# A kernel that plans its own order: from one planned order to twelve, each with banks and slots given by the one before

## The chip, the cores and the metric

The kernel runs on one core of one Trainium2 chip. A core has a matrix engine (TensorE, PE in the profile, with its weight loads listed apart as PEld), a vector engine (VectorE, DVE), a scalar engine (ScalarE, ACT), a general engine (GpSimd, POOL) and a synchronising engine (SP), which here issues the transfers between the main memory and the core's own memory. Each engine works through its own list of instructions in order and waits on semaphores for the others. Matrix products land in a small accumulator memory, PSUM, which has eight banks; everything else lies in SBUF.

The metric is the time of one execution on the device, in microseconds (us). The kernel before took 1474.14 us in the median of three runs (1473.09 to 1474.48).

## What is computed

A trunk of four residual layers over a sequence of 256 positions with 1024 channels. Each layer is a token mixer followed by a gated feed-forward layer (SwiGLU). The mixers are, in order, RWKV-7 time mixing, stick-breaking attention, sparse attention over selected keys (DSA), and RWKV-7 once more.

```python
for i in range(DEPTH):                     # DEPTH = 4
    kind, j = i % N_MIXERS, i // N_MIXERS  # N_MIXERS = 3
    h = rms_norm(x, norm_mix[i])
    if kind == 0:
        y, v_layer = rwkv7_time_mix(h, v_first, ...)
    elif kind == 1:
        y = stick_breaking_attention(h, sb_w_qkv[j], sb_w_out[j])
    else:
        y = dsa_attention(h, ds_w_in[j], ds_q_norm[j], ds_k_norm[j], ds_w_out[j])
    x = x + y
    x = x + swiglu(rms_norm(x, norm_ffn[i]), ffn_w_gu[i], ffn_w_down[i])
```

In the sparse attention a small indexer scores the keys for each query, the 64 best visible ones are kept, and an ordinary softmax attention with 16 heads runs over these alone. In RWKV-7 each head carries a 64 by 64 state through time:

```python
sa = einsum('bhvk,bhk->bhv', state, kk_t)
state = state * w_t - sa[..., None] * (kk_t * a_t) + v_t[..., None] * k_t
y_t = einsum('bhvk,bhk->bhv', state, r_t)
```

## The kernel before

The activations stay on the core, channels on the 128 partitions and the 256 positions along the free dimension. All weights come in 397 pieces of 128 by 1024 numbers (512 KB each), loaded into four rotating slots (`raw`). In most layers a piece is split on arrival into a rounded high part (`wh`, a cast on ScalarE or VectorE) and the rest (`wl`, a subtraction on VectorE). The products then run on the rounded halves: a pass with `wh` over the high and the low half of the activations, and one with `wl` over the high half. RWKV's r, k and v products use the unsplit piece.

The feed-forward layer makes 22 gate and 22 up products (`gate`, `up`), then eight products back to 1024 channels (`dn`). The RWKV layer makes its r, k and v products (`rp`, `kp`, `vp`), small products for its gates (`lora_in`, `lw`, `la`, `g1a`, `g1b`, `pg`), scores within chunks of 64 positions (`sc`), the inverse of a triangular matrix per head and chunk, finished by many 32 by 32 products (`cmb`), and then the recurrence over four chunks (`xu`, `qu`, `pS`, `Y`, with the state in `Sn`); the output product is `po`. The sparse attention makes the index products (`qi`, `kiwi`), keys of the index (`ki`), scores (`idx`), picks the best 64 on VectorE by eight rounds of "take the eight greatest, strike them out", and then treats eight pairs of heads: projection (`qk`), norm (`qss`), rotation (`qrot`), masked scores (`z`), softmax, transposition (`pT`), the weighted sum (`attn_o`). Value products (`vps`) and output products (`po`) are spread among them.

Nothing of this is issued directly. The layers are written as calls on a recording object, `Plan`: `record` (line 318) makes an operation (`Op`, line 179) with an estimated cost per engine, and finds from the overlap of regions in each buffer which earlier operations it needs. Some operations may go to either of two engines (`any`: a copy to ScalarE or VectorE, a product of two SBUF tiles to VectorE or GpSimd). Several matmuls may form one unit. At the end `emit` (line 650) calls `schedule` (line 630) and issues the instructions in the planned order. All instructions issued through it carry line 661, so the profile's groups are told apart by the names of their tiles.

`_prepare` (line 377) gives buffers of a group with a fixed number of slots (`ps`, five PSUM banks; `g`, two; `t`, twelve small tiles; `wh` and `wl`, three each; and single places such as `SB` or `s6`) their slot. It walks the buffers in the order in which the program recorded them, and gives each the slot whose last user stands earliest in that recorded order. The first operations on the new buffer then depend on all last reads and writes of the old one. The groups `raw` and `xm` (`FREE`, line 221) are left to the scheduling itself. Then it adds loads of ScalarE's function tables, and gives each operation a rank: its cost and the longest chain of costs and latencies behind it.

`_schedule` (line 420) is a list scheduler. It keeps a time per engine, takes the engine that can start first, and of its ready operations the one of highest rank, with some exceptions (`choose`, line 508): an engine waits for a more urgent operation that is about to be ready, goes elsewhere with an operation that another engine would finish sooner, and keeps TensorE for a while on products of one shape class, the full array or parts of it (operations whose `parts` flag is set have 64 rows or columns or fewer; a change costs `SWITCH`). Where the plan has TensorE waiting, it puts in filler (`keep_warm`, line 480): pairs of small bf16 products `warm_o` from a constant tile (`WARMERS = 2`, line 215). They compute nothing that is used; they hold the matrix engine's clock up. How many are put in follows from a count of the array's recent columns (`filled`).

In the kernel before one order is made. The `reserve` values are tried in turn until one gives a complete order.

Of the kernel before, what the change touches and what calls it, by code (L numbers as in the profile page):

```python
# [61 lines left out]
class Region:  # L62


    def __init__(self, p0, p1, cols, width):
        self.p0, self.p1 = p0, p1
        cols = np.asarray(cols).ravel()
        self.lo, self.hi = int(cols.min()), int(cols.max()) + 1
        self.mask = None
        if len(cols) < self.hi - self.lo or len(np.unique(cols)) < self.hi - self.lo:  # L70
            self.mask = np.zeros(width, bool)
            self.mask[cols] = True
# [106 lines left out]
class Op:  # L179


    def __init__(self, eng):
        self.eng, self.instrs, self.cost, self.table, self.cols = eng, [], 0.0, None, 0.0
        self.preds, self.succs, self.alts, self.warmer, self.parts = set(), [], {}, False, False
        self.bufs, self.ns = [], 0.0


class Queue:
# [27 lines left out]
ROW = 3  # L216
GAP = 1100.0
RESERVES = (1, 2, 3, 4, 5, 6)

WAIT = {"tensor": 85.0, "vector": 55.0, "scalar": 40.0, "gpsimd": 40.0, "sync": 0.0}  # L220
FREE = ("raw", "xm")
# [58 lines left out]
class Plan:  # L280
# [95 lines left out]

    def _prepare(self, counts):

        for b in self.bufs:
            if b.ops:  # L380
                b.ops = list(dict.fromkeys(b.ops))
                b.first, b.last = min(o.idx for o in b.ops), max(o.idx for o in b.ops)
        self.grouped, held = {}, {}
        for b in sorted((b for b in self.bufs if b.ops and b.group is not None), key=lambda b: b.first):
            if b.group in FREE:
                self.grouped.setdefault(b.group, []).append(b)
                for o in b.ops:
                    o.bufs.append(b)
                continue
            slots = held.setdefault(b.group, [None] * counts.get(b.group, 1))  # L390
            k = min(range(len(slots)), key=lambda i: -1 if slots[i] is None else slots[i].last)
            old = slots[k]
            if old is not None:
                assert old.last < b.first, (b.name, old.name, b.group)
                for o in b.roots:
                    o.preds |= {q for q, _ in old.writes + old.reads if q is not o}
            slots[k], b.slot = b, f"{b.group}_{k}"
        load, table, now, before = None, None, [], []
        for o in list(self.ops):
            if o.table is None:  # L400
                continue
            if o.table != table:
                table, before, now = o.table, now, []
                load = Op("scalar")
                load.cost, load.table, load.idx = 1290.0, table, o.idx - 0.5
                load.preds |= set(before)
                self.ops.append(load)
            o.preds.add(load)
            now.append(o)
        self.ops.sort(key=lambda o: o.idx)  # L410
        for o in self.ops:
            o.preds.discard(o)
            for q in o.preds:
                assert q.idx < o.idx
                q.succs.append(o)
        for o in reversed(self.ops):
            o.base = o.eng, o.cost
            o.rank = o.cost + max((s.rank + self._lat(o, s) for s in o.succs), default=0.0)

    def _schedule(self, counts, reserve):  # L420
        engines = ("tensor", "vector", "scalar", "gpsimd", "sync")
# [206 lines left out]
        return max(free.values()), sorted(out, key=lambda o: o.start)  # L628

    def schedule(self, counts):  # L630
        self._prepare(counts)
        best = None
        for reserve in RESERVES:
            r = self._schedule(counts, reserve)
            if r is not None:
                best = r
                break
        self.time, self.out = best
        Plan.last = self
        return self.out  # L640

# [1087 lines left out]
```

## Time and profile before

| | before |
|---|---|
| median of three runs | 1474.14 us |
| the profiled execution | 1473.95 us |
| its span, from the first to the last instruction | 1472.2 us |
| mean granted TensorE clock | 0.999 |
| TensorE busy | 1447.0 us |
| filler products `warm_o` | 294 |
| read from main memory | 219.70 MB |

The profile is a page on one execution, together with views that answer narrower questions: groups of instructions with their busy time and mean duration, waits by releaser, the chain that ended last, a timeline, and busy times within chosen stretches. Two points help in reading them. Matmuls are pipelined, so the duration of one is longer than the time that it takes from its successor: a feed-forward product of 512 columns is listed with 398 ns, though the next starts earlier. The time of a sequence is therefore read from start to start. And a product on full-precision (f32) numbers appears as two records, so the profile counts 10434 matmuls where the program has 8498.

### The profile page before, as it was taken

How to read it: one execution, taken by the hardware profiler on the slowest of the kernel's cores; microseconds unless marked ns; L12 is line 12 of the kernel's file. 1: busy time of each engine (PE TensorE's matmuls, PEld its weight loads, DVE VectorE, ACT ScalarE, POOL GpSimd, SP SyncE). 2: the span in 40 equal slices, each digit the busy share in tenths (PEclk: the TensorE clock that was granted, in tenths of full speed). 3: DMA queues.
4: the chain of work that ended last, by engine and by line, in shares of the span. 5: the costliest groups of instructions: out<-in, count | busy, mean ns of one | idle time of the engine just before them, and what ended most of it. 6: DMA issues, size and time to landing. Idle time of an engine off the chain costs nothing.

```text
span 1472.2 us, 26233 instructions
## 1 busy us (share of the span) xinstructions
PE 1447.0 (98%) x10434; PEld 1228.1 (83%) x10434; DVE 1107.1 (75%) x2026; ACT 718.3 (49%) x1348; POOL 61.3 (4%) x57
## 2 busy tenths in 40 slices
PE   9999999999999999999999989999999999999998
PEld 6788788888888888888977868888877877888887
DVE  7297478998566779986789978986474884789864
ACT  2344665444447655444546755444325256654442
POOL 0000010000000010000100010000100001200000
PEclk9999999999999999999999999999999999999999
DMA  7234135655554445555634445555523430455653
GB/s 254 91 107 144 36 101 172 194 183 194 175 183 136 130 158 186 198 187 181 192 113 130 129 144 172 186 193 183 197 93 108 129 101 18 130 175 182 196 188 132
DMA packets 77803, 224.55 MB, mean 153 GB/s; under 512 B 23536, under 2 KB 23792, under 8 KB 77424
## 3 DMA queue, kind: packets, MB, share of 16 engines
q1 hardware_dynamic: 77680, 222.87, 46.4%
q8 instruction: 82, 1.34, 0.4%
q14 instruction: 41, 0.34, 0.1%
HBM read 219.70 MB, written 3.15 MB: 151 GB/s over the span
## 4 chain that ended last, share of the span: by engine, by line
PE 86%; DVE 9%; ACT 2%; DMA 2%; issue 1%; SPq 0%; POOL 0%; DVEq 0%
PE up L661 17%; PE dn L661 16%; PE gate L661 16%; PE qk L661 5%; PE po L661 4%; PE kp L661 4%; PE rp L661 4%; PE vps L661 3%; PE z L661 2%; DVE wl L661 2%; PE vp L661 2%; PE warm_o L1564 1%; PE Y L661 1%; PE sc L661 1%; DVE xg L661 1%
## 5 line engine op out<-in xcount | busy, mean ns | idle before, releaser
L661 ACT CAST wh<-raw 128x1024 fp32r<-128x1024 f32 x317 | 329.7, 1050 | 401.8 <-PE dn L661 130.2
L661 DVE TENSOR_TENSOR wl<-raw,wh 128x1024 fp32r<-128x1024 f32 x349 | 420.3, 1222 | 70.0 <-ACT wh L661 58.5
L661 PE MATMUL gate<-xg,wh 128*128 128x512 f32 x704 | 259.9, 398 | 3.9 <-DVE xg L661 2.1
L661 PE MATMUL up<-xg,wh 128*128 128x512 f32 x704 | 259.9, 397 | 0.0
L661 PE MATMUL dn<-h,wh 128*128 128x512 f32 x704 | 247.6, 394 | 0.0
L661 PE MATMUL dn<-h,wl 128*128 128x256 f32 x704 | 197.5, 280 | 0.0
L661 PE MATMUL gate<-xg,wl 128*128 128x256 f32 x704 | 197.2, 280 | 0.0
L661 PE MATMUL up<-xg,wl 128*128 128x256 f32 x704 | 197.2, 280 | 0.0
L661 PEld LDWEIGHTS gate<-xg,wh 128*128 128x128 f32 x704 | 132.2, 188 | 38.1 <-DVE xg L661 3.4
L661 PEld LDWEIGHTS up<-xg,wh 128*128 128x128 f32 x704 | 132.2, 188 | 31.1
L661 PEld LDWEIGHTS dn<-h,wh 128*128 128x128 f32 x704 | 132.4, 188 | 30.8
L661 PEld LDWEIGHTS up<-xg,wl 128*128 128x128 f32 x704 | 132.8, 189 | 0.2
L661 PEld LDWEIGHTS gate<-xg,wl 128*128 128x128 f32 x704 | 132.8, 189 | 0.1
L661 PEld LDWEIGHTS dn<-h,wl 128*128 128x128 f32 x704 | 132.4, 188 | 0.0
L661 PE MATMUL qk<-xg,wh 128*128 128x256 f32 (+1 forms) x384 | 95.0, 326 | 0.1
L661 PE MATMUL qk<-xg,wl 128*128 128x256 f32 x256 | 72.0, 281 | 0.4 <-DVE wl L661 0.4
L661 PEld LDWEIGHTS qk<-xg,wh 128*128 128x128 f32 x384 | 64.2, 189 | 7.8 <-issue 1.4
L661 PE MATMUL kp<-pre,raw 128*128 128x256 f32 x256 | 59.9, 386 | 1.7 <-DVE pre L661 1.7
L661 DVE TENSOR_TENSOR gus<-gus,rstd 128x512 f32<-128x512 f32 x88 | 59.8, 687 | 1.2
L661 PE MATMUL vp<-xv,raw 128*128 128x256 f32 x256 | 59.0, 385 | 0.9 <-DVE vf L661 0.9
L661 PE MATMUL rp<-xr,raw 128*128 128x256 f32 x256 | 58.7, 382 | 0.0
L661 PEld LDWEIGHTS kp<-pre,raw 128*128 128x128 f32 x256 | 47.3, 190 | 13.3 <-issue 4.0
(292 smaller groups left out, 2355.5 us busy)
## 6 DMA issues: line engine op xcount, KB each, us to landing
raw<-in_wts_dram SPq DMA_DIRECT2D x397, 512.0 KB, 3.6
lora<-in_lora_dram SPq DMA_DIRECT2D x2, 1536.0 KB, 9.2
lg<-in_lora_dram SPq DMA_DIRECT2D x4, 512.0 KB, 5.4
xt<-in_xT_dram SPq DMA_DIRECT2D x4, 256.0 KB, 4.0
lora<-in_lora_dram SPq DMA_DIRECT2D x2, 512.0 KB, 5.6
xi<-in_id_dram SPq DMA_DIRECT2D x2, 512.0 KB, 8.0
scr<-SB SPq DMA_DIRECT2D x8, 128.0 KB, 3.4
xa<-scr SPq DMA_DIRECT2D x2, 512.0 KB, 3.3
```

Source lines behind the costliest of these rows:

```text
L661: getattr(getattr(nc, o.eng), method)(*map(real, args), **{k: real(a) for k, a in kw.items()})
L1564: lambda: [nc.tensor.matmul(wo[:, :S], wx[:, :P], wx, start=True, stop=True) for _ in range(WARMERS)])
```

## The change

`_prepare` no longer gives slots. It only collects the buffers that share a group, and keeps for each operation the needs that come from the data (`needs`) and its first engine and cost (`base`). A new function, `_place`, takes an order, sorts the buffers of each group by their first use in that order, and gives each the slot whose old buffer is finished earliest by the planned end times (`end`) of that order. It then makes the dependencies and ranks anew. `schedule` starts from the recorded order with made-up times, so that its first round gives slots as before. It repeats placing and scheduling `ROUNDS = 12` times, each round starting from the order of the round ahead of it without its fillers. By the planner's own estimate of the total time it keeps the shortest of the twelve, and restores engines, costs, instructions, times and slots of that one.

```diff
+ROUNDS = 12
...
+    def _place(self, counts, order):
+
+        at = {o: i for i, o in enumerate(order)}
+        for o in self.ops:
+            o.preds, o.succs = set(o.needs), []
+        for g, bufs in self.grouped.items():
+            bufs.sort(key=lambda b: min(at[o] for o in b.ops))
+        for g, bufs in self.placed.items():
+            slots = [None] * counts.get(g, 1)
+            for b in sorted(bufs, key=lambda b: min(at[o] for o in b.ops)):
+                k = min(range(len(slots)), key=lambda i: -1.0 if slots[i] is None else max(o.end for o in slots[i].ops))
+                old = slots[k]
+                if old is not None:
+                    for o in b.roots:
+                        o.preds |= {q for q, _ in old.writes + old.reads if q is not o}
+                slots[k], b.slot = b, f"{g}_{k}"
+        for o in self.ops:
+            o.preds.discard(o)
             for q in o.preds:
-                assert q.idx < o.idx
+                assert at[q] < at[o]
                 q.succs.append(o)
-        for o in reversed(self.ops):
-            o.base = o.eng, o.cost
-            o.rank = o.cost + max((s.rank + self._lat(o, s) for s in o.succs), default=0.0)
+        for o in reversed(order):
+            o.rank = o.base[1] + max((s.rank + self._lat(o, s) for s in o.succs), default=0.0)
...
     def schedule(self, counts):
         self._prepare(counts)
-        best = None
-        for reserve in RESERVES:
-            r = self._schedule(counts, reserve)
-            if r is not None:
-                best = r
-                break
-        self.time, self.out = best
+        order, best = self.ops, None
+        for o in order:
+            o.start, o.end = o.idx, o.idx + 0.5
+        for _ in range(ROUNDS):
+            self._place(counts, order)
+            for reserve in RESERVES:
+                r = self._schedule(counts, reserve)
+                if r is not None:
+                    break
+            if best is None or r[0] < best[0]:
+                best = r + ([(o.eng, o.cost, o.instrs, o.start, o.end) for o in r[1]], [b.slot for b in self.bufs])
+            order = [o for o in r[1] if not o.warmer]
+        self.time, self.out = best[:2]
+        for o, state in zip(best[1], best[2]):
+            o.eng, o.cost, o.instrs, o.start, o.end = state
+        for b, slot in zip(self.bufs, best[3]):
+            b.slot = slot
```

The arithmetic, the numbers of slots and banks, the cost estimates and the transfers stay as they are.

More of the change, by code (lines that the diff above doesn't have):

```diff
@@ L184, in __init__ @@
         self.preds, self.succs, self.alts, self.warmer, self.parts = set(), [], {}, False, False
-        self.bufs, self.ns = [], 0.0
+        self.bufs, self.ns, self.end = [], 0.0, 0.0
 class Queue:
@@ L377, in _prepare @@
     def _prepare(self, counts):
+        self.grouped, self.placed = {}, {}
         for b in self.bufs:
@@ L382, in _prepare @@
                 b.first, b.last = min(o.idx for o in b.ops), max(o.idx for o in b.ops)
[L383 to L397, printed above, removed]
+                if b.group in FREE:
+                    self.grouped.setdefault(b.group, []).append(b)
+                    for o in b.ops:
+                        o.bufs.append(b)
+                elif b.group is not None:
+                    self.placed.setdefault(b.group, []).append(b)
         load, table, now, before = None, None, [], []
@@ L412, in _prepare @@
             o.preds.discard(o)
+            o.needs, o.base = frozenset(o.preds), (o.eng, o.cost)
+    def _place(self, counts, order):
[15 more added lines that the diff above has]
+            o.preds.discard(o)
             for q in o.preds:
-                assert q.idx < o.idx
+                assert at[q] < at[o]
                 q.succs.append(o)
-        for o in reversed(self.ops):
-            o.base = o.eng, o.cost
-            o.rank = o.cost + max((s.rank + self._lat(o, s) for s in o.succs), default=0.0)
+        for o in reversed(order):
+            o.rank = o.base[1] + max((s.rank + self._lat(o, s) for s in o.succs), default=0.0)
     def _schedule(self, counts, reserve):
```

## The prediction

> **What bounds the kernel now.** I read the page first, then busy time by stage, then the filler passes by stage, then TensorE's waits and its timeline. The page says whose time it is.
>
> ```profile
> span 1472.2 us, 26233 instructions
> PE 1447.0 (98%) x10434; PEld 1228.1 (83%) x10434; DVE 1107.1 (75%) x2026; ACT 718.3 (49%) x1348; POOL 61.3 (4%) x57
> PE 86%; DVE 9%; ACT 2%; DMA 2%; issue 1%; SPq 0%; POOL 0%; DVEq 0%
> ```
>
> TensorE (PE) is busy nearly always and holds 86% of the chain that ended last. But part of that busy time computes nothing: the passes named warm_o, which the planner puts where its own plan has TensorE waiting. Cut at the first gate product and the last dn product of each feed-forward layer, the span has eight stages; five are shown (RWKV, a feed-forward layer, stick-breaking, sparse attention, RWKV):
>
> ```profile
> core 0: us, PE busy (x) PEld busy (x) DVE busy (x) ACT busy (x) POOL busy (x), PEclk, DMA share, GB/s
> 1.20:219.40 218.20, 214.28 (x2134) 172.03 (x2135) 142.57 (x358) 103.17 (x277) 12.09 (x13) 1.00 0.38 123
> 219.40:407.20 187.80, 187.19 (x1062) 162.69 (x1063) 152.05 (x223) 88.66 (x114) 6.18 (x4) 1.00 0.56 184
> 407.20:525.70 118.50, 117.76 (x786) 101.98 (x783) 82.61 (x136) 75.13 (x148) 3.45 (x3) 1.00 0.46 147
> ...
> 712.50:876.20 163.70, 155.80 (x1139) 133.74 (x1137) 138.62 (x282) 97.57 (x218) 9.68 (x8) 1.00 0.43 138
> ...
> 1070.90:1280.80 209.90, 206.88 (x2097) 165.94 (x2097) 144.02 (x370) 99.43 (x269) 9.95 (x10) 1.00 0.31 94
> ```
>
> The same stretches for warm_o alone:
>
> ```profile
> 1.20:219.40 218.20, 20.02 (x126) 1.00 0.38 123
> ...
> 712.50:876.20 163.70, 8.17 (x64) 1.00 0.43 138
> 876.20:1070.90 194.70, 4.26 (x36) 1.00 0.55 184
> 1070.90:1280.80 209.90, 10.81 (x64) 1.00 0.31 94
> ```
>
> The reader is to see two kinds of stage. A feed-forward layer has TensorE full (187.19 of 187.80 us) without filler: no order can shorten it. The sparse attention loses most: 8.17 us of filler and 163.70 - 155.80 = 7.9 us idle. The two RWKV stages hold 126 and 64 filler passes; the first 64 of the 126 stand ahead of the first product, while inputs load.
>
> **The change part by part.** It adds and removes no arithmetic; it changes the order, the banks and slots, and the engine of some copies. With one order instead of twelve the new planner gives exactly the old program, so all that follows comes from the later orders. In the changed kernel's instruction order (the fifth of the twelve; counts below are from it) the matmuls are the same but for warm_o, 236 instead of 294. Per stage: first RWKV 126 to 120, sparse attention 64 to 26, last RWKV 64 to 50, all others equal. The four feed-forward stages have the same sequence of products as before.
>
> *Filler.* Per pass, from the rows above: 8.17/64 = 0.128 us in the sparse attention, 10.81/64 = 0.169 in the last RWKV, 20.02/126 = 0.159 in the first. So 38 x 0.128 + 14 x 0.169 + 6 x 0.159 = 4.9 + 2.4 + 1.0 = 8.2 us. Back to back a pass takes less, about 3.88/34 = 0.114 us:
>
> ```profile
> 1.19 5.73 PE L1564 MATMUL warm_o<-warm_x 128*128 128x256 bf16 x30 [1.19 <-DVE eps_rms L661]
> 9.21 3.88 PE L1564 MATMUL warm_o<-warm_x 128*128 128x256 bf16 x34
> 20.36 3.72 PE L661 MATMUL kp<-pre,raw 128*128 128x256 f32 x16
> 24.01 1.08 PE L661 MATMUL lora_in<-xm,lora 128*64 128x256 f32 x8
> 25.02 1.99 PE L661 MATMUL kp<-pre,raw 128*128 128x256 f32 x8
> 26.95 1.08 PE L661 MATMUL lora_in<-xm,lora 128*64 128x256 f32 x8
> ```
>
> That makes the lower end 58 x 0.114 = 6.6 us. I take 8.2, because the removed passes mostly stood in pairs between dependent products, not in long runs.
>
> *Switches between the full array and parts of it.* 16 kp passes hold TensorE from 20.36 to 24.01 (3.65 us), 8 from 25.02 to 26.95 (1.93): 1.72 for eight more, 0.215 each, so each visit carries 1.93 - 8 x 0.215 = 0.21 us beside its passes, 0.10 for each of its two switches. The order before has 280 switches, the new one 246: first RWKV 108 to 102, sparse attention 38 to 34, last RWKV 110 to 86. 34 x 0.10 = 3.4 us. The lower end is nothing (a switch made while waiting is free). I take 3.4: in RWKV most switches stand amid a busy TensorE.
>
> *Waits in the sparse attention.* What TensorE waited for there, longest four:
>
> ```profile
> PE qrot L661 <- DVE rhl L661: 2.7, 4, 1.7
> PE vps L661 <- DVE wl L661: 1.5, 1, 1.5
> PE pT L661 <- DVE prs L661: 1.0, 1, 1.0
> PE qss L661 <- ACT prs L661: 0.9, 1, 0.9
> ```
>
> They stand beside the filler at two places: from the index keys (ki) to the first masked score product (z), and around the last two head pairs.
>
> ```profile
> 745.37:775.38 30.01, 26.37 (x188) 21.87 (x188) 28.82 (x84) 13.44 (x22) 1.59 (x3) 1.00 0.26 89
> 851.44:868.24 16.80, 13.84 (x96) 9.39 (x95) 8.52 (x25) 9.49 (x32) 0.00 (x0) 1.00 0.43 158
> 851.44:868.24 16.80, 5.03 (x40) 1.00 0.43 158
> 729.58 0.72 PE qk L661 x6
> 781.59 1.38 PE vps L661 x6
> ```
>
> In the first stretch VectorE (DVE) is busy 28.82 of 30.01 us with the top-k; TensorE has only 96 qk and 24 vps passes to put beside it (96 x 0.12 + 24 x 0.23 = 17.0 us). The new order has 240 qk and 48 vps passes there (39.8 us): later head pairs are projected early, so the pairs overlap afterwards. At the end, where 40 of the 64 filler passes stood, the new order has 4: output products (po) stand between the last pairs. The four rows make 6.1 us of waits, and I count them down as the filler falls, by 38/64: 3.6 us. Bounds: 0 (the same waits elsewhere) and all 6.1.
>
> *New waits.* No row shows the new order's own. The nearest is what the old planner left unfilled: 3.9 us idle in the first RWKV (218.20 - 214.28) up to 7.9 in the sparse attention. A new order may leave less as well as more; after the term above I bound it by -3.9 and +7.9 and take +3, since the new order packs the chains closer and a late link then stalls sooner.
>
> *Engine choices.* VectorE loses 7 weight casts to ScalarE and 5 rotary products to GpSimd:
>
> ```profile
> L661 DVE CAST wh<-raw 128x1024 fp32r<-128x1024 f32 x32 | 23.0, 719 | 10.4 <-PE vps L661 5.4 <-PE qk L661 2.6 <-PE xu L661 1.7
> L661 ACT CAST wh<-raw 128x1024 fp32r<-128x1024 f32 x317 | 329.7, 1050 | 401.8 <-PE dn L661 130.2
> L661 DVE TENSOR_TENSOR qk<-qa,sbt 128x512 f32<-128x512 f32 x5 | 3.5, 692 | 0.2
> L661 POOL TENSOR_TENSOR qk<-qa,sbt 128x512 f32<-128x512 f32 x3 | 4.3, 1428 | 49.2 <-DVE qa L661 42.5 <-PE qk L661 6.7
> L661 DVE TENSOR_TENSOR wl<-raw,wh 128x1024 fp32r<-128x1024 f32 x38 | 46.9, 1238 | 4.4 <-ACT wh L661 4.2
> L661 DVE TENSOR_TENSOR qa<-qk,rstd 128x512 f32<-128x512 f32 x8 | 5.4, 681 | 0.3 <-PE qk L661 0.2
> ...
> 762.54 1.30 POOL L661 TENSOR_TENSOR qk<-qa,sbt 128x512 f32<-128x512 f32 x1 [6.70 <-PE qk L661]
> 762.71 1.68 DVE L661 CAST wh<-raw 128x1024 fp32r<-128x1024 f32 x1
> ```
>
> Each cast is 0.33 us slower, each product 0.74 us. I cost them at nothing: ScalarE is busy 97.57 of 163.70 us in that stage, and the product runs beside the split, rotation and sine product of the same pair. Uncovered they cost 7 x 0.33 + 5 x 0.74 = 6.0 us. There is a second price: the cast that began 0.17 us after a GpSimd product took 1.68 us, not 0.72, about 1.0 us late. Five more such products hold VectorE up by at most 5.0 us and spare it 5 x 0.692 = 3.5: 1.5 more VectorE time, which I leave to the rival below.
>
> "SBUF — State Buffer" of the Trainium skill, under "SBUF: two separate sides", has the reason: VectorE in a two-port mode or with two SBUF inputs and GpSimd hold that pair exclusively for a whole instruction, and the other blocks. By that rule each product may cost VectorE its full 1.43 us, 3.7 us net for five; the pair of rows agrees in kind.
>
> DMA issues are the same in number; where one moves, the DMA share (0.31 to 0.56) leaves room.
>
> *The sum.* 1472.2 - 8.2 - 3.4 - 3.6 + 3.0 = 1460.0 us of span. The profiled run took 1473.95, 1.75 outside the span; the median of the runs shown is 1474.14, 0.2 above it. Forecast 1462.0 us. Its own range: all 6.1 us of waits gone and no new ones gives 1456; filler at 6.6, no gain from switches or waits, and the 3 us lost gives 1470.5.
>
> **The rivals.**
>
> *VectorE takes over in the sparse attention (slower).* The first stretch gets 144 more qk passes (six weight pieces) and 24 more vps passes (two pieces): eight splits of 1.238 us and three evictions of 0.681 on VectorE, 28.8 + 11.9 = 40.7 us, against TensorE's 39.8. For it: VectorE is already full there, the mask stands behind all of that on its queue, and GpSimd's five products delay it by 1.5 us more. Against it: the work is only moved ahead, and the stage's total on VectorE (138.62 of 163.70) falls. It decides once the mask is later than the prefilled products; then pairs run on their own chain as the last two did, 16.80 us with 13.84 - 5.03 = 8.8 of work, 8.0 us lost per two pairs. Twice that on top of the forecast is 1478.
>
> *Waits stay, filler goes.* The removed passes leave idle time of the same length: only part of the switches remains, 1472. For it: filler alone never sets a time. Against it: the work between dependent products visibly changes.
>
> *The recurrences gain too.* The new order starts the state recurrence (xu, qu, pS, Y) amid the inverse's products (cmb) instead of behind most of them. In this stretch of the first RWKV:
>
> ```profile
> 150.00:172.00 22.00, 22.00 (x509) 16.12 (x511) 6.94 (x21) 13.71 (x52) 0.00 (x0) 1.00 0.11 39
> 150.00:172.00 22.00, 9.02 (x54) 1.00 0.11 39
> ```
>
> 9.02 of 22 us is filler, hiding latency. Half of it saved in both layers is 9 us more: 1453. Against it: the new order still holds 50 fillers in the last RWKV.
>
> *The clock falls.* Fewer fillers could cost clock. The first 30 passes took 5.73 us, 0.19 each, against 0.114 later: a cold stretch of that length costs 5.73 - 30 x 0.114 = 2.3 us, and six of them eat the gain, 1475. Against it: every stage shows 1.00, across waits of up to 1.7 us. "TensorE: Matmul & The Clock Gate" of the Trainium skill, under "What's actually happening", has the clock halved after an idle window of about 3.4 us; no wait here is as long.
>
> That the change does nothing is out: the sequences differ.
>
> **How the numbers follow.** Forecast 0.64, VectorE 0.11, waits stay 0.11, recurrences 0.12, clock 0.02. The range reaches below to just under the recurrences' 1453 and above past "waits stay" to the clock's 1475: 1452 to 1475, leaving out most of VectorE and the tails. A difference of 0.2% (2.9 us) is what a measurement of this kernel tells from none. Faster: forecast 0.63, recurrences 0.12, a third of "waits stay" 0.04: 0.79. Same: the rest of "waits stay" and a piece of VectorE and of the forecast: 0.11. Slower: 0.10.
>
> **What would show it.** Right: feed-forward stages at 187 us again, the sparse attention near 153, the last RWKV some 5 us shorter, clock 1.00 throughout. Wrong: the sparse attention's TensorE idle above 8 us with VectorE near 95% of it; an RWKV stage longer than before; or the filler gone with idle time grown by as much.

## The result, and the profile after

The changed kernel takes 1464.55 us in the median of six runs (1462.82 to 1465.98), against 1474.31 for the kernel before on the same chip (1473.09 to 1475.66): a ratio of 0.9932, 95% interval 0.9919 to 0.9945. The forecast was 1462.0 in a range of 1452 to 1475. The page of the changed kernel begins like this:

```profile
span 1462.9 us, 26102 instructions
PE 1440.6 (98%) x10376; PEld 1222.8 (84%) x10376; DVE 1104.9 (76%) x2034; ACT 720.2 (49%) x1334; POOL 70.6 (5%) x63
PE 88%; DVE 8%; ACT 2%; issue 1%; DMA 1%; SPq 0%; POOL 0%; DVEq 0%; ACTq 0%
```

The span is 9.3 us shorter, and TensorE bounds it as before. Busy times cut at the same events (columns: length, then busy time and count of PE, PEld, DVE, ACT and POOL, granted clock, DMA share, GB/s) show where:

```profile
1.20:217.30 216.10, 213.74 (x2128) 170.69 (x2129) 144.05 (x362) 102.16 (x273) 12.84 (x13) 1.00 0.38 125
...
405.10:523.70 118.60, 117.91 (x785) 102.03 (x783) 84.27 (x139) 75.30 (x145) 3.44 (x3) 1.00 0.46 147
...
710.50:866.90 156.40, 150.54 (x1101) 130.26 (x1099) 130.39 (x270) 102.24 (x225) 18.39 (x13) 1.00 0.44 145
...
1062.10:1271.60 209.50, 205.81 (x2082) 165.14 (x2083) 146.29 (x380) 96.94 (x258) 9.82 (x11) 0.99 0.31 94
```

The sparse attention fell from 163.7 to 156.4 us and gives four fifths of the gain. The first RWKV fell by 2.1, the last by only 0.4; stick-breaking and the feed-forward layers stayed within 0.5. The filler products alone, in the stages where they changed:

```profile
1.20:217.30 216.10, 19.95 (x120) 1.00 0.38 125
...
710.50:866.90 156.40, 3.36 (x26) 1.00 0.44 145
...
1062.10:1271.60 209.50, 7.87 (x50) 0.99 0.31 94
```

Over the whole span filler went from 44.0 to 36.2 us. TensorE's idle time went from 25.2 (1472.2 - 1447.0) to 22.3 (1462.9 - 1440.6). What is left, TensorE busy with real products, rose from 1403.0 to 1404.4. So -7.8 - 2.9 + 1.4 = -9.3. The rise stands in the last RWKV, shown here in three parts, before and after: from its first product to the first score product (`sc`), on to the first product of the inverse (`cmb`), and on to its end. First the kernel before:

```profile
1070.90:1143.60 72.70, 72.68 (x360) 55.28 (x360) 44.25 (x112) 28.16 (x72) 0.90 (x1) 1.00 0.30 95
1143.60:1211.90 68.30, 67.25 (x671) 54.75 (x670) 57.91 (x164) 26.37 (x69) 0.00 (x0) 1.00 0.39 115
1211.90:1280.80 68.90, 66.95 (x1071) 55.92 (x1069) 41.87 (x96) 44.90 (x128) 9.04 (x9) 1.00 0.23 71
```

Then the changed kernel:

```profile
1062.10:1136.70 74.60, 74.43 (x364) 54.88 (x364) 46.69 (x118) 28.67 (x72) 1.12 (x1) 1.00 0.30 92
1136.70:1205.90 69.20, 67.53 (x665) 55.38 (x664) 55.75 (x156) 27.69 (x72) 0.00 (x0) 0.98 0.38 114
1205.90:1271.60 65.70, 63.85 (x1054) 54.87 (x1055) 43.84 (x108) 40.58 (x115) 8.69 (x10) 1.00 0.24 74
```

The beginning of the first part on the changed kernel's TensorE timeline (start, duration):

```profile
1063.92 0.38 PE L1589 MATMUL warm_o<-warm_x 128*128 128x256 bf16 x2
1064.13 2.13 PE L686 MATMUL kp<-pre,raw 128*128 128x256 f32 x8
1066.10 0.38 PE L1589 MATMUL warm_o<-warm_x 128*128 128x256 bf16 x2
1066.41 0.65 PE L686 MATMUL lora_in<-xm,lora 128*64 128x256 f32 x4
1067.05 1.13 PE L686 MATMUL kp<-pre,raw 128*128 128x256 f32 x4
1068.11 0.65 PE L686 MATMUL lora_in<-xm,lora 128*64 128x256 f32 x4
1068.69 1.13 PE L686 MATMUL kp<-pre,raw 128*128 128x256 f32 x4
```

The recurrence at the end gained 3.2 us. The first part, where TensorE hardly waits, lost 1.9: four fillers that were not there before, and `lora_in` products mostly in groups of four passes where the old order had groups of eight, each group paying two changes of array mode. The middle lost 0.9 us, and its clock column reads 0.98. Two stretches of it, of 3.4 us each:

```profile
1167.69:1171.11 3.42, 3.42 (x8) 2.76 (x9) 3.35 (x12) 3.40 (x10) 0.00 (x0) 0.50 0.05 19
1171.11:1174.52 3.41, 3.41 (x17) 3.00 (x17) 3.13 (x9) 0.73 (x1) 0.00 (x0) 1.00 0.00 0
```

In the first the granted clock is half, and 8 products stand in it instead of 17: the profiled execution lost some 1.7 us there (3.42 x 0.5, an estimate). With these set aside real products fell by about 0.3 us instead of rising by 1.4, and the middle lost nothing through its order. At its end stands TensorE's longest wait of the stage, on VectorE (us, times, longest):

```profile
PE cmb L686 <- DVE xd L686: 1.2, 1, 1.2
```

### The profile page after: what moved, and what is told of

The parts are those of the page before. It is cut to its first block, busy times and chain, and to the rows that moved or that the text cites. A ratio compares the mean times of both kernels' runs of the same rounds, so it can differ in the third digit from the quotient of the medians.

```text
span 1462.9 us, 26102 instructions
## 1 busy us (share of the span) xinstructions
PE 1440.6 (98%) x10376; PEld 1222.8 (84%) x10376; DVE 1104.9 (76%) x2034; ACT 720.2 (49%) x1334; POOL 70.6 (5%) x63
## 4 chain that ended last, share of the span: by engine, by line
PE 88%; DVE 8%; ACT 2%; issue 1%; DMA 1%; SPq 0%; POOL 0%; DVEq 0%; ACTq 0%
PE up L686 17%; PE dn L686 17%; PE gate L686 16%; PE qk L686 5%; PE vp L686 4%; PE rp L686 4%; PE kp L686 4%; PE vps L686 3%; PE po L686 3%; PE z L686 2%; DVE wl L686 2%; PE sc L686 1%; DVE xg L686 1%; PE Y L686 1%; PE warm_o L1589 1%
## 5 line engine op out<-in xcount | busy, mean ns | idle before, releaser
L686 ACT CAST wh<-raw 128x1024 fp32r<-128x1024 f32 x324 | 338.1, 1050 | 415.3 <-PE dn L686 130.3
L686 PE MATMUL kp<-pre,raw 128*128 128x256 f32 x256 | 63.4, 389 | 2.0 <-DVE pre L686 1.7
```

The costliest lines, as they stand in the source:

```text
L686: getattr(getattr(nc, o.eng), method)(*map(real, args), **{k: real(a) for k, a in kw.items()})
```

## The experiments

My theory going in: the planner now needs less waiting, above all in the sparse attention, and the fillers mark how much. Its rival: the filler products themselves cost the time, so that any kernel with fewer of them is faster. The kernel before ran beside each of the following on the same chip; the ratios and intervals are to those runs.

### Is filler idle time, or does it delay?

Edits, in the changed kernel (`half_after`, `none_after`) and in the kernel before (`half_before`, `none_before`):

```diff
-              lambda: [... for _ in range(WARMERS)])
+              lambda: [... for _ in range(WARMERS // 2)])                        # half
+              lambda: [... for _ in range(WARMERS if next(calls) < 32 else 0)])  # none after the start
```

> The order before, with one filler product where the plan has two (147 instead of 294; 63 of the 147 removed stand ahead of the first weight product). Theory 1, filler only stands where TensorE would wait anyway: within 2 us of the kernel before (1474.3). Theory 2, filler itself delays the products behind it, and the change gained because it issues fewer: the 84 passes removed after the start save 0.114 us each, 9.6 us, about 1465.

> The changed order with one filler product for two (118 instead of 236, 58 of the removed after the start). Theory 1 (filler only fills): within 2 us of the changed kernel's 1464.6. Theory 2 (filler delays): 58 x 0.114 = 6.6 us less, about 1458.

> The changed order with only the 64 fillers ahead of the first weight product. Theory 1 (filler only fills, and the clock holds without it): within 2 us of 1464.6. Theory 2 (filler delays): 172 passes x 0.114 = 19.6 us less, about 1445. Theory 3 (filler holds the clock): granted clock below 1.00 in the RWKV stages, products there up to twice as long, over 1475.

> The order before with only the 64 fillers ahead of the first weight product. Theory 1 (filler only fills): within 2 us of 1474.3. Theory 2 (filler delays): 230 x 0.114 = 26 us less, about 1448. Theory 3 (clock): over 1480, clock below 1.00 in the RWKV stages.

Measured: half_before 1472.2 us (0.9973, 0.9955 to 0.9991), half_after 1467.39 (0.9944, 0.9926 to 0.9963), none_after 1471.66 (0.9970, 0.9954 to 0.9987), none_before 1474.59 (0.9993, 0.9977 to 1.0009). No single theory holds; none_before lands on theory 1's figure, but with the clock at 0.981 to 0.984 in all ten executions, so that two effects cancel, and half_after, at 0.989 to 0.996, is no faster than the changed kernel. The stretch from the first `cmb` product to the end of the stage tells the parts from each other. Before, then half_before, first RWKV:

```profile
150.50:219.40 68.90, 67.00 (x1070) 55.97 (x1069) 40.34 (x92) 44.72 (x128) 9.05 (x9) 1.00 0.20 63
```

```profile
151.30:217.40 66.10, 63.91 (x1040) 53.97 (x1038) 40.12 (x92) 44.72 (x128) 9.04 (x9) 1.00 0.21 65
```

Thirty fillers fewer at the same clock are 2.8 us, 0.093 each. Here filler does delay: the product behind it would have been ready sooner. But the order without any filler lost the clock in both recurrences. none_after, its two recurrences, and then TensorE's waits in the first of them (us, times, longest):

```profile
150.00:200.00 50.00, 48.08 (x857) 40.89 (x856) 23.71 (x67) 28.88 (x99) 2.98 (x4) 0.76 0.11 34
...
1210.00:1272.00 62.00, 58.95 (x941) 51.76 (x942) 37.35 (x99) 35.84 (x105) 7.41 (x9) 0.78 0.19 55
```

```profile
PE vb L686 <- ACT ysq L686: 0.5, 1, 0.5
PE xu L686 <- DVE u L686: 0.5, 2, 0.3
PE xu L686 <- ACT XT L686: 0.5, 1, 0.5
```

Over the same first stretch the clock is 0.76 although TensorE is busy 48.08 of 50 us and never waits longer than 0.5 us. Most of its products there are small (32 by 32, 64 by 64). So filler in the recurrences buys the clock, and costs just under 0.1 us a pass where the clock holds with fewer. In the sparse attention it is otherwise. half_after has 13 fillers there instead of 26, at the full clock:

```profile
709.70:866.10 156.40, 149.12 (x1087) 128.95 (x1086) 130.40 (x270) 102.14 (x225) 18.40 (x13) 1.00 0.46 144
```

The stage takes 156.40 us, as in the changed kernel; what filler lost, idle time gained (7.3 us against 5.9). There filler only fills, and the changed kernel's gain is not that of fewer fillers. half_before can't show this for the old order: its sparse attention took 166.2 us (710.4 to 876.6) against 163.7, but with the clock at 0.96.

### Filler halved in one recurrence only

> The changed kernel, with one filler product for two only in the first RWKV stage from the first inverse product on (25 fewer, 211 in all); everything else as it is. Theory 2, in the recurrence filler delays what stands behind it, at 0.1 us a pass as half_after showed between the first cmb product and the end of the stage (66.3 to 63.7 us with the clock at 1.00): that stretch near 63.7, the kernel 2.6 us below the changed one, about 1462. Theory 1, filler only fills: stretch 66, 1464.6.

```diff
+              lambda: [... for _ in range(1 if 35 <= next(calls) < 60 else WARMERS)])
```

The profiled execution leans to theory 2: from its first `cmb` product at 150.6 us the stage ended at 215.5, 64.9 us, against 66.8 in the changed kernel, 1.9 us of the 2.6 expected. The kernel did not gain. Twelve executions gave a median of 1470.29 (0.9965, 0.9942 to 0.9987) and fall into two groups: six of 1464.6 to 1466.6 at a granted clock of 0.996 to 0.998, six of 1474.0 to 1476.9 at 0.988 to 0.990. The same program keeps the clock in half of its executions. In none of the six of the changed kernel was it below 0.998, but six are few: the kernel before, run beside these experiments, fell to 0.989 to 0.991 (1485 to 1488 us) in five of the 76 executions that the ratios rest on.

### Are the twelve orders told apart by their fillers?

Each of the first three runs takes one given order instead of the shortest by estimate (`stick400` keeps the choice and sets `STICK = 400.0`):

```diff
-            if best is None or r[0] < best[0]:
+            if _ == 1:    # order2; 2 for order3, 10 for order11
```

> The second of the twelve orders, taken whatever the planner estimates (248 fillers; sparse attention 26, last RWKV 56). Theory A, the gain follows the planned waiting that the fillers mark, 9.8 us per 58 passes or 0.17 us each: 46 fewer, 1466.5. Theory B, the orders differ on the chip without regard to their fillers: anywhere from 1462 to 1476.

> The third order (282 fillers; sparse attention 40, both RWKV stages 202 against 190 before). Theory A: 12 fewer, 1472.3, with the sparse attention 4 us shorter and RWKV 2 longer. Theory B: anywhere from 1462 to 1476.

> The eleventh order (236 fillers like the one kept, but split as 118, 22 and 56 over first RWKV, sparse attention and last RWKV). Theory A: 1464.5, the same as the changed kernel. Theory B: anywhere from 1462 to 1476.

> The changed kernel with STICK 400 in place of 1000: the planner gives up an array mode for a smaller gain in rank; another set of twelve orders, the kept one with 206 fillers (106 in the first RWKV, 12 in the sparse attention, 48 in the last RWKV) against 236. Theory A, the time follows the planned waiting: 30 fewer at 0.17 us, 1459.5. Theory B, fillers of a kept order tell little: within 3 us of 1464.6 on either side.

Measured: order2 1465.35 (0.9943, 0.9913 to 0.9973), order3 1475.04 (0.9992, 0.9960 to 1.0024), order11 1466.78 (0.9930, 0.9905 to 0.9955), stick400 1465.26 (0.9926, 0.9904 to 0.9948). Of order3's ten executions five had a clock of 0.987 to 0.991 and took 1479 to 1483 us; the other five took 1468 to 1471. Theory A is near for order2 and order11, and wrong for stick400: 30 fillers fewer than the changed kernel gave nothing. For order3 its 1472.3 lies between the two groups, and the stages don't follow it: the sparse attention, forecast 4 us shorter, took 153.5 us with 40 fillers, 10 shorter. In order2 the sparse attention is this:

```profile
715.30:868.00 152.70, 150.12 (x1100) 130.43 (x1098) 128.78 (x267) 103.41 (x229) 15.95 (x12) 1.00 0.46 148
```

With 26 fillers there, like the changed kernel with its 156.4 us, it takes 152.7, the least of all profiled runs, and gives that back in the first RWKV (220.1 against 216.1). Among orders that place by use, filler counts do not tell a few microseconds apart. The choice among twelve shows no gain over the second order alone that these runs can tell; order2 lost clock in two of its ten executions (0.985 and 0.990), the changed kernel in none of six.

### Banks or slots?

```diff
+            use = g in ("ps", "g")        # banks_only; "not in" for slots_only
+            for b in sorted(bufs, key=lambda b: min(at[o] for o in b.ops) if use else b.first):
+                k = min(range(len(slots)), key=lambda i: -1.0 if slots[i] is None else
+                        max(o.end for o in slots[i].ops) if use else slots[i].last)
```

> Only the PSUM banks (groups ps and g) are placed by the order ahead; all SBUF slots by the recorded order as before; again the shortest of twelve (238 fillers; sparse attention 20, RWKV 124 and 54). If the banks carry the gain: 1465, the sparse attention near 156. If the SBUF slots carry it: 1473 or more.

> Only the SBUF slots (t, wh, wl and the single places) and the turn of raw and xm follow the order ahead; PSUM banks by the recorded order as before (300 fillers: 128 first RWKV, 64 sparse attention, 68 last RWKV; before had 126, 64 and 64). If the banks make the sparse attention shorter: that stage near 163, the kernel 1472 to 1476. If the slots do: near 156, below 1468.

Measured: banks_only 1470.36 (0.9981, 0.9945 to 1.0017; span 1467.6), slots_only 1472.09 (0.9974, 0.9962 to 0.9986; span 1469.4). Two of banks_only's ten executions lost the clock (0.987 and 0.984, 1485.6 and 1489.2 us); the other eight took 1468.9 to 1472.0, so that its 1465 was missed by either count. The sparse attention, and the weighted sums of its head pairs (shortest, middle and longest duration in ns, then first and last start), banks_only first:

```profile
715.50:871.60 156.10, 149.07 (x1095) 129.42 (x1093) 132.24 (x271) 100.51 (x224) 19.45 (x13) 1.00 0.47 145
```

```profile
L688 PE MATMUL attn_o<-sbt x64: 272/326/431, 818.6 to 860.9; 128*64 128x256 f32 x32, 128*64 128x128 f32 x32
```

Now slots_only:

```profile
711.30:875.00 163.70, 155.91 (x1139) 133.76 (x1137) 138.54 (x282) 97.50 (x218) 9.67 (x8) 1.00 0.44 138
1069.70:1277.90 208.20, 206.51 (x2101) 164.99 (x2101) 143.67 (x367) 100.54 (x271) 9.24 (x11) 1.00 0.32 95
```

```profile
L688 PE MATMUL attn_o<-sbt x64: 272/326/431, 783.5 to 865.9; 128*64 128x256 f32 x32, 128*64 128x128 f32 x32
```

And the same row of the kernel before, then of the changed kernel:

```profile
L661 PE MATMUL attn_o<-sbt x64: 272/326/430, 784.6 to 867.0; 128*64 128x256 f32 x32, 128*64 128x128 f32 x32
L686 PE MATMUL attn_o<-sbt x64: 272/326/430, 806.7 to 856.2; 128*64 128x256 f32 x32, 128*64 128x128 f32 x32
```

The banks carry the sparse attention alone (in both runs the turn of `raw` and `xm` follows the order ahead; the banks without that were not run). With them placed by use the weighted sums of all eight pairs fit into 42 us (50 in the changed kernel), with banks by the recorded order they take 82, as before. In the kernel before each pair's scores (`z`) begin only behind the start of the weighted sum of the pair ahead: scores from 775.3, 788.2 and 800.8 us, weighted sums from 784.6, 798.3 and 807.4, and so on. In the changed kernel the scores of all eight pairs have begun at 843.5, when four of the weighted sums have. The SBUF slots are worth something in RWKV instead: 1.2 us in the first (217.0) and 1.7 in the last. In banks_only the first RWKV took 220.9 us, 2.7 more than before; that keeps its gain small, and by its interval the whole kernel's gain is not told from none. That an early pair's bank was tied to the last use of the pair recorded ahead of it is how I read this; no run shows the tie itself.

### Does GpSimd hold VectorE up?

```diff
+            eng, instrs = o.eng, o.instrs
+            if eng == "gpsimd" and "vector" in o.alts and instrs[0][1][0].buf.name == "qk":
+                eng, instrs = "vector", [o.alts["vector"][0]]
```

> The changed order, with the eight rotary products that the planner gave to GpSimd in the sparse attention issued on VectorE in their place. If GpSimd holds VectorE up for as long as it spares it: the sparse attention within 0.5 us of 156.3, the kernel within 1.5 us of 1464.6, VectorE's other instructions of that stage shorter (prs scaling back from 0.51 to 0.31 us in the mean). If the move to GpSimd was a gain: 8 x 0.69 = 5.5 us more on VectorE, the stage 2 to 5 us longer.

Measured: 1463.27 us (0.9911, 0.9891 to 0.9932). Groups of that stage in the changed kernel:

```profile
L686 DVE TENSOR_TENSOR qk<-qk,qa 128x512 f32<-128x512 f32 x8 | 6.2, 771 | 0.0
L686 DVE TENSOR_SCALAR prs<-prs,sm 128x128 f32<-128x128 f32 (+1 forms) x13 | 6.3, 507 | 0.0
...
L686 POOL TENSOR_TENSOR qk<-qa,sbt 128x512 f32<-128x512 f32 x8 | 12.7, 1593 | 45.6 <-DVE qa L686 34.5 <-DVE sm L686 11.1
```

The stage (from 710.60 us in this run) and the groups with the products on VectorE:

```profile
710.60:866.40 155.80, 150.31 (x1100) 130.30 (x1099) 130.37 (x278) 102.16 (x225) 5.65 (x5) 1.00 0.47 145
```

```profile
L689 DVE TENSOR_TENSOR qk<-qk,qa 128x512 f32<-128x512 f32 x8 | 5.4, 681 | 0.0
L689 DVE TENSOR_TENSOR qk<-qa,sbt 128x512 f32<-128x512 f32 x8 | 5.4, 679 | 0.0
L689 DVE TENSOR_SCALAR prs<-prs,sm 128x128 f32<-128x128 f32 (+1 forms) x13 | 3.6, 300 | 0.0
```

Eight more products (5.4 us) left VectorE's busy time where it was, 130.37 against 130.39 us, and the stage is 0.6 us shorter: what GpSimd spared VectorE, it took back, above all by stretching the softmax scaling from 300 to 507 ns in the mean and the sum of the rotation from 681 to 771. The stretched ones are few: in the changed kernel three of the 13 scalings took 0.9 to 1.3 us and one of the eight sums 1.4, and each of these began while a GpSimd product ran. This fits the shared port pair of "SBUF — State Buffer" of the Trainium skill, under "SBUF: two separate sides"; the rows agree. The run has the fastest median of the study, but its interval overlaps that of the changed kernel.

## Why the prediction was right, and by how much

**Time, sign and place.** 1464.55 against 1462.0. The sparse attention was to come near 153 and came to 156.4; the feed-forward layers were to stay and did; the last RWKV was to lose some 5 us and lost 0.4; the clock was to be 1.00 throughout and was 0.99 in that stage. That the total came so near is in part luck: one term failed and another made up for half of it.

**Filler.** 8.2 forecast, 7.8 measured over the span. In the sparse attention the term is exact (4.9 forecast, 8.17 - 3.36 = 4.8); in the first RWKV 1.0 was forecast and 0.1 came, in the last 2.4 and 2.9. The reading of it needs a correction: that fewer fillers shorten the kernel was right here because the new order needed less waiting there. Taking filler out of an order is not the same, as the first experiments show.

**Switches: the step that failed.** "34 x 0.10 = 3.4 us" counted every change of array mode, those into and out of a filler pair among them. Such a pair, in the recurrence of the kernel before:

```profile
153.48 0.44 PE L661 MATMUL cmb<-XT,zs 32*32 32x32 f32 x16
153.86 0.39 PE L1564 MATMUL warm_o<-warm_x 128*128 128x256 bf16 x2
154.18 0.44 PE L661 MATMUL cmb<-xd,SB 32*32 32x32 f32 x16
```

From its start to that of the next product are 0.32 us, where two passes back to back take 0.23: the price of 0.169 us a pass, 0.34 a pair, held one of its two changes already. Without filler, counted as the prediction counts them, the sequences have 66 and 66 changes in the first RWKV, 38 and 34 in the sparse attention, 66 and 64 in the last RWKV: six fewer, not 34. And they moved to a worse place: in the first part of the last RWKV, where TensorE is never short of work, 29 became 33 (31 in the first RWKV). The price was too low as well: it took the overhead of the `kp` visit, 0.21 us, for both switches, but eight `lora_in` passes took 1.01 us and four take 0.58, which leaves 0.15 beside them, so that a switch costs nearer 0.18 (an estimate from these rows). Real products took 1.4 us more instead of 3.4 less. Of the 4.8 us between, 1.7 is the half clock shown above, which the prediction had not at all; the other 3.1 are this term: with the clock set aside real products took 0.3 us less, not 3.4.

**Waits.** Forecast: 3.6 us less in the sparse attention, 3.0 new ones. Measured: idle time there from 7.9 to 5.9, first RWKV from 3.9 to 2.4, last RWKV from 3.0 to 3.7, over the span 2.9 less. The sum was 2.3 us better than forecast and hid half of the 4.8. The longest four after, in the sparse attention:

```profile
PE qk L686 <- DVE qa L686: 1.2, 1, 1.2
PE qrot L686 <- DVE rhl L686: 1.0, 1, 1.0
PE qss L686 <- ACT prs L686: 0.9, 1, 0.9
PE pT L686 <- DVE prs L686: 0.7, 1, 0.7
```

**Engine choices.** Costed at nothing, with 1.5 us more of VectorE time by the port: rotary_on_vector bears out that the move of the products was no gain, and VectorE's busy time was the same with it and without. The seven moved casts were not tested.

**The rivals.** VectorE did not take over: it is busy 130.39 of 156.40 us, 83% as against 85%. "Waits stay" is out: idle time fell with the filler. The recurrences did gain, 2.1 us in the first RWKV and 3.2 in the last, where the first part of the stage took 1.9 of it back. The clock fell a little: one stretch at half clock in the profiled execution, 1.7 us against the 2.3 that the rival put on a cold stretch, and 0.998 or more in all six. But the reason given against that rival was wrong: it argued from the length of waits, and none_after lost the clock in its first recurrence with no wait above 0.5 us. Orders of the same twelve lost more of it (order2 in two of ten executions, order3 in five).

## What to carry to other kernels

Where a scheduler may reorder work but memory is handed out in program order, the memory order can quietly undo the reordering; placing PSUM banks by the planned use let eight chains overlap that had run nearly one behind the other. When two terms of a sum are counted from the same sequence, remove from the second what the first has already priced: count switches with the filler left out. And an order that a plan calls shorter should be read by stage: this one gained in a recurrence and gave more than half of it back in a part that had nothing to wait for.

## What the runs showed of the hardware that was not expected

The granted clock falls without a long wait. With no filler it was 0.76 and 0.78 in the two recurrences, with TensorE listed as busy 96% and 95% of the stretch. Busy is not full, since listed durations overlap: in the rows of the filler pair above, sixteen 32 by 32 products are all begun within 0.38 us, from 153.48 to 153.86, though each is listed with 194 ns in the mean. In all the traces of this case the clock is either whole or half, and a half stretch that ends within the span lasts 3.41 us or a multiple of it: that long in the changed kernel, seven times as long (23.9 us) in the first recurrence of none_after. "TensorE: Matmul & The Clock Gate" of the Trainium skill, under "What's actually happening", names an idle window as what lowers it; here it fell in stretches of mostly small products too. Between the extremes it is a matter of the single execution: halving the filler in one recurrence left six executions of twelve at 0.996 to 0.998 and six at 0.988 to 0.990, some 10 us apart. What decides it in one execution is open.
